# Norms, residuals and low parts of an fp32 encoder step on VectorE alone, with a norm's shift taken from its first tile and four gates moved into the projection

## The chip, the cores and the metric

The kernel runs on one core of a Trainium2 chip. Times are device microseconds of one launch on that core; the kernel before takes 1536.71 us (median of three runs, 1534.43 to 1537.71). Five engines matter: TensorE (PE, matmuls; PEld is its weight load), VectorE (DVE), ScalarE (ACT), GpSimd (POOL) and SyncE (SP, whose queue issues the loads and stores). They run side by side and wait for one another through semaphores; each takes its own instructions in the order in which the program has them.

## The reference

Two layers (DEPTH = 2) work on 320 tokens (64 of a running stream, 256 of a new one) of width 1024, all in fp32. Each layer is

```
x <- LN1(ALPHA*x + 0.5*FFN1(x))            FFN: silu(x @ w1a) * (x @ w1g) @ w2, hidden width 2816
z  = x @ w_in                              latent q, latent kv, rotary key, band q/k/v, gate_a, gate_b
A  = latent attention of z (8 heads), B = banded attention of z (8 heads)
mix = (sigmoid(gate_a)*(A @ w_proj_a) + sigmoid(gate_b)*(B @ w_proj_b)) @ w_out
x <- LN2(ALPHA*x + mix)
x <- LN3(ALPHA*x + 0.5*FFN2(x))
```

LN subtracts the mean over the 1024 features, divides by the root of the variance plus EPS, and applies a gain and a bias. The outputs are x and the new keys and values of both attentions.

## The kernel before, in words

Activations lie transposed: 1024 features are KD = 8 tiles of 128 partitions, the T = 320 tokens are columns. Every fp32 matmul of the weights is made of three products of a faster 32-bit type, fp32r: each operand is split into a high part (a rounded copy) and a low part (operand minus high part), and `mm3` (L126) adds hi x hi, hi x lo and lo x hi in PSUM.

Weights come as 383 chunks of 8 blocks (128x128 each), in the order in which the program asks for them (`WeightStream`, L49). SP loads a chunk of 512 KB into one of three staging buffers. `_split` (L71) makes the high part on ScalarE (L81) and the low part (L83), in pieces of 512 columns: every sixth low piece on GpSimd, the others on VectorE. There are four split buffers, and splits are asked for two chunks ahead. One chunk feeds 24 products.

A feed-forward stage (`ffn`, L255) makes 22 hidden tiles: two PSUM banks each, `evac` forms silu(a)*g, ScalarE its high part and GpSimd its low part (L276). Then `produce` (L290) makes the eight output tiles, which go straight into the norm.

`layer_norm` (L304) adds residual and product to eight tiles d. To keep the sum of squares accurate it first takes a shift c from all tiles: the mean over the features of the first NS = 4 tiles, through a matmul with a matrix of ones (pc, L369). After tile 4 (NB = 5) the shift is subtracted from the five tiles already there (L377); later tiles get it with their residual (L360). S collects the sum of the tiles (L347), Q the sum of squares (L353). GpSimd adds the halves of x (L315), scales them (L317) and does most of S and Q; VectorE the rest. For each finished tile `make_raw` (L323) forms high and low part of d times gain (L326, L327), because the next stage begins with the unnormalised tile: `group` opens six PSUM banks of the next stage, `step` adds one tile's products to all six, and the finished sums are corrected afterwards with mean and deviation (`finish`, L243). After the first `step` the sums of S and Q over partitions are two fp32 matmuls (pm, pq, L388 and L389); ScalarE and VectorE make the deviation (L398 to L405); GpSimd subtracts the mean from the eight tiles (L428), VectorE scales (L429), ScalarE writes the high part of the new x (L430) and VectorE the low part (L435, tile 7 on GpSimd). The last norm has no next stage; there the tiles go out to y (L407 to L421).

The mixer (`mixer`, L439; class `Mixer`, L469) has the banded attention first, then the latent one, head pair by head pair: `mla_scores` and `values` (L573). `M.run` (L115) gives the score and value products priority and keeps them in order among themselves. `gate` (L783) makes one tile of a gate: eight blocks of weights, 24 products, a tanh on ScalarE. `pb` (L885) multiplies gate b with a projected tile of the banded attention, whose outputs are the tiles ob. The outputs oa of the latent attention have the same tags (`o{n}{i}`, one buffer each, L840 and L906). `project` (L929) projects oa, multiplies with gate a, adds the gate b part and splits the sum; `w_out` and the norm follow. Tag K (keys, NK = 6 buffers) is shared by the banded keys, the latent keys, two pairs of gate a tiles (`gpair`, L788) and raw tiles of the norm.

PSUM has two tags, "mm" and "at", of four banks each. The order of instructions on every engine is not the order of the program: a planner (`schedule_with_timeline_sim`, L1050) runs the program on its own model of the engines' costs and gives each engine, at each time, the earliest instruction of the program that is ready in that model. Buffers are taken when their first writer is placed and are free when the last reader is done.

Of the kernel before, what the change touches and what calls it, by code (L numbers as in the profile page):

```python
# [14 lines left out]
P = 128  # L15
# [21 lines left out]
NK = 6  # L37
# [11 lines left out]
class WeightStream:  # L49


    def __init__(self, nc, dram, stage_pool, split_pool, ahead_dma, ahead_split):
        self.nc, self.dram = nc, dram
        self.sp, self.pp = stage_pool, split_pool
        self.ad, self.asp = ahead_dma, ahead_split
        self.order = []
        self.loaded = {}
        self.split = {}
        self.nl = self.ns = self.nlo = 0
# [11 lines left out]
    def _split(self):  # L71
# [6 lines left out]
        half = CH * P // (4 if c == 0 else 2)  # L78
        for a in range(0, n, half):
            b = min(n, a + half)  # L80
            self.nc.scalar.copy(hi[:, a:b], t[:, a:b])  # L81
            self.nlo += 1
            (self.nc.gpsimd if self.nlo % 6 == 0 else self.nc.vector).tensor_tensor(lo[:, a:b], t[:, a:b], hi.bitcast(F32)[:, a:b], ALU.subtract)  # L83
# [18 lines left out]
class Model:  # L102
# [152 lines left out]
    def ffn(self, l, f, pre):  # L255
# [3 lines left out]
        with tc.tile_pool(name="h", bufs=1, reuse_waits="tile") as hp, \  # L259
# [4 lines left out]
            def evac(p, pa, pg, raw):  # L264
# [11 lines left out]
                self.lo(hl[p], h, hh[p], eng=nc.gpsimd)  # L276
# [20 lines left out]
            tiles = [rp.tile([P, T], F32, name=f"d{m}") for m in range(KD + 3)]  # L297
# [4 lines left out]
            return self.layer_norm(l, which, tiles, raw, produce, 0.5, group)  # L302

    def layer_norm(self, l, which, tiles, raw, produce, ys, group):  # L304
# [4 lines left out]
        d, (c, S, Q) = tiles[:KD], tiles[KD:]  # L309
        NS, NB = 4, 5  # L310
        cg = l * NC_L + C_LN[which]
        cr = self.rr.tile([P, T], F32R, tag="cr", name="cr")

        def base(m):
            nc.gpsimd.tensor_tensor(d[m], self.xhi[m].bitcast(F32), self.xlo[m].bitcast(F32), ALU.add)  # L315
            if m < NB and ys != 1.0:
                nc.gpsimd.tensor_scalar(d[m], d[m], ALPHA, None, ALU.mult)  # L317
            if not last:
# [4 lines left out]
        def make_raw(m):  # L323
            if not last:
                g = self.cst[:, cg + 2 * m:cg + 2 * m + 1]
                nc.scalar.activation(raw[m][0][:, :T], d[m], AF.Copy, scale=g)  # L326
                nc.vector.scalar_tensor_tensor(raw[m][1][:, :T], d[m], g, raw[m][0].bitcast(F32)[:, :T], ALU.mult, ALU.subtract)  # L327

        def add(m, ps):
            if ys != 1.0:  # L330
                nc.vector.scalar_tensor_tensor(d[m], ps, ys, d[m], ALU.mult, ALU.add)
            elif m < NB:
                nc.vector.scalar_tensor_tensor(d[m], d[m], ALPHA, ps, ALU.mult, ALU.add)
            else:
                nc.vector.tensor_tensor(d[m], d[m], ps, ALU.add)  # L335

        def accumulate(m, ps):
            if m == KD - 1:
                if last:
                    nc.scalar.activation(sq, d[m], AF.Square)  # L340
                    return
                if ys != 1.0:
                    nc.vector.scalar_tensor_tensor(S, ps, ys, S, ALU.mult, ALU.add)
                else:
                    nc.vector.tensor_tensor(S, S, ps, ALU.add)
            elif m:
                nc.gpsimd.tensor_tensor(S, d[0] if m == 1 else S, d[m], ALU.add)  # L347
            if m == 0:
                nc.scalar.activation(Q, d[0], AF.Square)
            else:  # L350
                q = self.scratch("sq")
                nc.scalar.activation(q, d[m], AF.Square)
                (nc.gpsimd if m < NB else nc.vector).tensor_tensor(Q, Q, q, ALU.add)  # L353

        sq = self.scratch("sq") if last else None
        for m in range(KD):
            base(m)
        for m in range(KD):
            if m >= NB:
                nc.vector.scalar_tensor_tensor(d[m], d[m], ALPHA, c, ALU.mult, ALU.subtract)  # L360
                if m == KD - 1 and not last:
                    nc.gpsimd.tensor_tensor(S, S, d[m], ALU.add)
# [4 lines left out]
            if m == NB - 1:  # L367
                pc = self.psum("at", "pc")
                self.mm(pc[:, :T], self.ones if last else self.onesr, c if last else cr, True, True)  # L369
                nc.scalar.activation(c, pc[:, :T], AF.Copy, scale=float(KD) / NS)  # L370
            add(m, ps[:, :T])
            if m < NB:
                if 1 <= m < NS:
                    nc.gpsimd.tensor_tensor(cr if m == NS - 1 and not last else c, d[0] if m == 1 else c, d[m], ALU.add)
                if m == NB - 1:
                    for j in range(NB):
                        nc.vector.tensor_tensor(d[j], d[j], c, ALU.subtract)  # L377
                        accumulate(j, None)
                        make_raw(j)
            else:  # L380
                make_raw(m)
                accumulate(m, ps[:, :T])
        if not last:
# [4 lines left out]
        self.mm(pm[:, :T], self.ones, S, True, not last)  # L388
        self.mm(pq[:, :T], self.ones, Q, True, not last)  # L389
        if last:  # L390
            self.mm(pm[:, :T], self.ones, d[KD - 1], False, True)
# [7 lines left out]
        if last:  # L399
            nc.vector.scalar_tensor_tensor(v, pq[:, :T], EPS, msq, ALU.add, ALU.subtract)  # L400
        else:
            nc.vector.tensor_tensor(v, pq[:, :T], msq, ALU.subtract)
            nc.vector.tensor_scalar(v, v, 0.0, EPS, ALU.max, ALU.add)
        nc.scalar.activation(v, v, AF.Sqrt)
        nc.vector.reciprocal(v, v)  # L405
        if last:
            nc.scalar.copy(md, pm[:, :T])  # L407
            for m in (7, 2, 5, 6, 4, 0, 1, 3):
# [654 lines left out]
```

## Time and profile before

| | |
|---|---|
| median of three runs | 1536.71 us |
| profiled execution | 1536.8 us, of which the span is 1535.0 |
| TensorE busy | 1492.3 us (97%), 10207 products |
| VectorE busy | 900.1 us (59%) |
| ScalarE busy | 744.3 us (48%) |
| GpSimd busy | 564.5 us (37%) |
| DMA | 219.46 MB, 143 GB/s |

In the profile a line such as `L83 DVE TENSOR_TENSOR wlo<-wst,whi 128x512 ... x640 | 468.3, 762 | 444.1 <-ACT whi L81 439.4` names the line of the kernel, the engine, the operation, output and inputs by the program's names, their shapes and the number of such instructions; then the busy time in us and the mean of one in ns; then the engine's idle time just before them and what ended most of it. Many helpers record all their instructions under one line (all products are L109), so tiles tell them apart. In the mixer's norm the tiles d go by the name gt, because they take the buffers of gate b. Idle time of an engine that nobody waits for costs nothing.

### The profile page before, as it was taken

The numbers are of one execution on the slowest core, as the hardware profiler recorded it, in microseconds if no ns is written. First come the engines' busy times: TensorE is split into PE (matmuls) and PEld (weight loads), VectorE is DVE, ScalarE is ACT, GpSimd is POOL, SyncE is SP. The second block draws the span as 40 slices with busy tenths as digits, with TensorE's granted clock in tenths as the row PEclk, the third lists the DMA queues.
The fourth block names the chain that finished last, engine by engine and source line by source line (L and its number), as shares of the span: only waits on it lengthen the run. The fifth ranks groups of instructions, "written<-read, shape, count | busy, mean of one in ns | idle before, by whom it ended". The sixth has DMA issues, their size and how long they took to land. (4 is left out here: it accounts for less than half of the span.)

```text
span 1535.0 us, 26682 instructions
## 1 busy us (share of the span) xinstructions
PE 1492.3 (97%) x10207; PEld 1454.5 (95%) x10207; DVE 900.1 (59%) x1587; ACT 744.3 (48%) x1563; POOL 564.5 (37%) x602
## 2 busy tenths in 40 slices
PE   9999999999999899999999999999999998999996
PEld 9999999999898899999999999998998998999996
DVE  6333368675566994333884333786655579833345
ACT  5444345765453554443554443467645545544332
POOL 7322145332004683222483222452220156722234
PEclk9999999999999999999999999999999999999998
DMA  7545435844323435444434454458342333444441
GB/s 225 164 151 151 151 124 167 248 144 132 97 87 98 147 107 171 148 152 151 148 114 164 141 154 148 138 171 241 110 150 87 97 120 116 148 154 152 151 138 62
DMA packets 69921, 219.46 MB, mean 143 GB/s; under 512 B 8417, under 2 KB 17569, under 8 KB 69793
## 3 DMA queue, kind: packets, MB, share of 16 engines
q1 hardware_dynamic: 69792, 217.75, 45.6%
q8 instruction: 80, 1.31, 0.3%
q14 instruction: 49, 0.39, 0.1%
HBM read 211.74 MB, written 4.67 MB: 141 GB/s over the span
## 5 line engine op out<-in xcount | busy, mean ns | idle before, releaser
L83 DVE TENSOR_TENSOR wlo<-wst,whi 128x512 fp32r<-128x512 f32 (+1 forms) x640 | 468.3, 762 | 444.1 <-ACT whi L81 439.4
L81 ACT CAST whi<-wst 128x512 fp32r<-128x512 f32 (+1 forms) x768 | 437.0, 617 | 469.3 <-PE ps L109 189.1
L109 PE MATMUL ps<-xlo,whi 128*128 128x320 f32 x1760 | 547.5, 312 | 6.0 <-DVE xlo L435 6.0
L109 PE MATMUL ps<-xhi,whi 128*128 128x320 f32 x1760 | 548.0, 313 | 3.9 <-DVE fin L250 3.2
L109 PE MATMUL ps<-xhi,wlo 128*128 128x320 f32 x1760 | 545.6, 312 | 3.5 <-POOL wlo L83 3.2
L83 POOL TENSOR_TENSOR wlo<-wst,whi 128x512 fp32r<-128x512 f32 x128 | 176.1, 1376 | 466.3 <-ACT whi L81 428.8
L109 PEld LDWEIGHTS ps<-xlo,whi 128*128 128x128 f32 x1760 | 332.9, 189 | 7.2 <-DVE xlo L435 6.5
L109 PEld LDWEIGHTS ps<-xhi,whi 128*128 128x128 f32 x1760 | 332.9, 190 | 5.9 <-issue 4.1
L109 PEld LDWEIGHTS ps<-xhi,wlo 128*128 128x128 f32 x1760 | 332.3, 189 | 5.0 <-POOL wlo L83 3.4
L109 PE MATMUL ps<-hh,whi 128*128 128x320 f32 x704 | 217.8, 309 | 0.0
L109 PE MATMUL ps<-hh,wlo 128*128 128x320 f32 x704 | 217.6, 309 | 0.0
L109 PE MATMUL ps<-hl,whi 128*128 128x320 f32 x704 | 217.5, 309 | 0.0
L146 POOL TENSOR_TENSOR hl<-h,hh 128x320 fp32r<-128x320 f32 x88 | 86.1, 983 | 194.1 <-ACT hh L139 194.1
L109 PEld LDWEIGHTS ps<-hh,whi 128*128 128x128 f32 x704 | 132.1, 188 | 0.1
L109 PEld LDWEIGHTS ps<-hl,whi 128*128 128x128 f32 x704 | 132.1, 188 | 0.1
L109 PEld LDWEIGHTS ps<-hh,wlo 128*128 128x128 f32 x704 | 132.2, 188 | 0.0
L274 DVE TENSOR_TENSOR h<-silu,ps 128x320 f32<-128x320 f32 x79 | 38.3, 486 | 71.3 <-PE ps L109 67.4
L139 ACT CAST hh<-h 128x320 fp32r<-128x320 f32 x88 | 40.2, 457 | 54.3 <-DVE h L274 44.0
L109 PE MATMUL ps<-raw,whi 128*128 128x322 f32 x192 | 44.7, 319 | 1.2 <-DVE raw L327 1.2
L109 PE MATMUL ps<-rawl,whi 128*128 128x322 f32 x144 | 45.5, 316 | 0.0
L347 POOL TENSOR_TENSOR d<-d,d 128x320 f32<-128x320 f32 x24 | 27.0, 1125 | 50.0 <-DVE d L377 29.3
L109 PE MATMUL ps<-rawh,wlo 128*128 128x322 f32 x144 | 45.2, 314 | 0.0
(271 smaller groups left out, 2061.7 us busy)
## 6 DMA issues: line engine op xcount, KB each, us to landing
wst<-in_w_dram SPq DMA_DIRECT2D x382, 512.0 KB, 3.6
K<-in_ckT_dram SPq DMA_DIRECT2D x8, 256.0 KB, 5.2
vc<-in_cv_dram SPq DMA_DIRECT2D x8, 256.0 KB, 5.1
T<-in_E_dram SPq DMA_DIRECT2D x16, 128.0 KB, 4.5
xin<-in_x_dram SPq DMA_DIRECT2D x8, 160.0 KB, 6.1
out_kb_dram<-K SPq DMA_DIRECT2D x8, 160.0 KB, 4.0
out_vb_dram<-vt SPq DMA_DIRECT2D x8, 160.0 KB, 5.1
out_y_dram<-d SPq DMA_DIRECT2D x8, 160.0 KB, 1.8
```

Of the source, the lines that this page charges most:

```text
L81: self.nc.scalar.copy(hi[:, a:b], t[:, a:b])
L83: (self.nc.gpsimd if self.nlo % 6 == 0 else self.nc.vector).tensor_tensor(lo[:, a:b], t[:, a:b], hi.bitcast(F32)[:, a:b], ALU.subtract)
L109: return self.nc.tensor.matmul(out, lhsT, rhs, start=start, stop=stop)
L139: self.nc.scalar.copy(out, src)
L146: eng.tensor_tensor(out, src, hi.bitcast(F32), ALU.subtract)
L274: nc.vector.tensor_tensor(h, s, pg[:, :T], ALU.mult)
L347: nc.gpsimd.tensor_tensor(S, d[0] if m == 1 else S, d[m], ALU.add)
```

## The change

- `_split`: pieces are whole chunks of 1024 columns (but for the first two chunks), and all low parts are made on VectorE.
- `ffn`: the low part of the hidden tiles is made on VectorE.
- The residual (sum of the halves of x) is a step of its own, `residual`, into one wide tile d: on VectorE in the feed-forward stages, on GpSimd in the mixer, where it now stands in the middle of the attention and has a buffer of its own.
- `layer_norm`: everything is scaled by 1/ys (2 in the feed-forward stages, with EPS scaled by 4). The shift is taken from tile 0 alone, right after it: one ScalarE copy, one product with the ones, one ScalarE copy of the result. All other residuals get the shift at once, and each tile adds its product later. Sums S and Q are made on VectorE. After the sums VectorE subtracts the mean from PSUM; in the last norm GpSimd does it for tiles 4, 5 and 6. Every tile's end is done the same way.
- The mixer: pb for tiles 4 to 7 stands after the values of pair 2 (before: right after the first scores). Gates a 4 to 7 are made in `project`, between its tiles; their buffers are five of one tag, and tag K has five buffers (NK = 5).

```diff
-        half = CH * P // (4 if c == 0 else 2)
-        for a in range(0, n, half):
-            b = min(n, a + half)
+        piece = CH * P // (4 if c == 0 else 2 if c == 1 else 1)
+        for a in range(0, n, piece):
+            b = min(n, a + piece)
             self.nc.scalar.copy(hi[:, a:b], t[:, a:b])
-            self.nlo += 1
-            (self.nc.gpsimd if self.nlo % 6 == 0 else self.nc.vector).tensor_tensor(lo[:, a:b], ...)
+            self.nc.vector.tensor_tensor(lo[:, a:b], t[:, a:b], hi.bitcast(F32)[:, a:b], ALU.subtract)
...
-                self.lo(hl[p], h, hh[p], eng=nc.gpsimd)
+                self.lo(hl[p], h, hh[p])
...
+    def residual(self, d, eng):
+        for m in range(KD):
+            eng.tensor_tensor(d[:, m * T:m * T + T], self.xhi[m].bitcast(F32), self.xlo[m].bitcast(F32), ALU.add)
...
+        ps = produce(0)
+        nc.vector.scalar_tensor_tensor(d[0], d[0], scale, ps[:, :T], ALU.mult, ALU.add)
+        nc.scalar.copy(cr, d[0])
+        pc = self.psum("at", "pc")
+        self.mm(pc[:, :T], self.onesr, cr, True, True)
+        nc.scalar.activation(c, pc[:, :T], AF.Copy, scale=float(KD))
+        for m in range(1, KD):
+            nc.vector.scalar_tensor_tensor(d[m], d[m], scale, c, ALU.mult, ALU.subtract)
+        nc.vector.tensor_tensor(d[0], d[0], c, ALU.subtract)
+        finished(0)
+        for m in range(1, KD):
...
             ps = produce(m)
+            if m == KD - 1:
+                nc.vector.tensor_tensor(S, S, d[m], ALU.add)
+                nc.vector.tensor_tensor(S, S, ps[:, :T], ALU.add)
+            nc.vector.tensor_tensor(d[m], d[m], ps[:, :T], ALU.add)
+            if m < KD - 1:
+                nc.vector.tensor_tensor(S, d[0] if m == 1 else S, d[m], ALU.add)
+            finished(m)
...
+        for m in range(KD):
+            if last and m in (4, 5, 6):
+                nc.gpsimd.tensor_tensor(d[m], d[m], md, ALU.subtract)
+            else:
+                nc.vector.tensor_tensor(d[m], d[m], pm[:, :T], ALU.subtract)
+        for m in (0, 1, 2, 3, 7, 4, 5, 6) if last else range(KD):
+            g, b = gain[m]
+            nc.vector.scalar_tensor_tensor(d[m], d[m], g, v, ALU.mult, ALU.mult)
...
         mscores(0)
-        for m in range(8):
+        for m in range(4):
             pb(m)
...
         mvalues(2)
-        for m in range(3, 8):
-            ga[m] = self.gate(0, m)
+        self.d = self.tile([P, KD * T], F32, "d")
+        M.residual(self.d, nc.gpsimd)
+        for m in range(4, 8):
+            pb(m)
+        ga[3] = self.gate(0, 3)
         mvalues(3)
...
         for m in range(8):
+            later = {1: 4, 2: 5, 4: 6, 6: 7}.get(m)
+            if later:
+                self.ga[later] = self.gate(0, later)
             ps = self.proj("pa", m, self.oa)
```

`finished(m)` holds what `make_raw` and the squares did: ScalarE's high part and VectorE's low part of d times gain, ScalarE's square, and its sum into Q on VectorE.

More of the change, by code (lines that the diff above doesn't have):

```diff
@@ L295, in produce @@
                 return ps
-            tiles = [rp.tile([P, T], F32, name=f"d{m}") for m in range(KD + 3)]
+            d = rp.tile([P, KD * T], F32, name="d")
+            sums = [rp.tile([P, T], F32, name=n) for n in ("c", "S", "Q")]
+            self.residual(d, nc.vector)
             raw = group = None
@@ L349, in accumulate @@
                 nc.scalar.activation(Q, d[0], AF.Square)
-            else:
+            elif not (last and m == KD - 1):
                 q = self.scratch("sq")
                 nc.scalar.activation(q, d[m], AF.Square)
[L353 to L362, printed above, removed]
+                nc.vector.tensor_tensor(Q, Q, q, ALU.add)
@@ L366, in layer_norm @@
             ps = produce(m)
[L367 to L383, printed above, removed]
+            if m == KD - 1:
[5 more added lines that the diff above has]
+            finished(m)
+        sq = None
+        if last:
+            sq = self.scratch("sq")
+            nc.scalar.activation(sq, d[KD - 1], AF.Square)
+        else:
             grp, step = group()
@@ new lines, in layer_norm @@
+        if not last:
+            for k in range(1, KD):
+                step(k, raw[k], TR)
+        for m in range(KD):
+            if last and m in (4, 5, 6):
+                nc.gpsimd.tensor_tensor(d[m], d[m], md, ALU.subtract)
+            else:
+                nc.vector.tensor_tensor(d[m], d[m], pm[:, :T], ALU.subtract)
+        for m in (0, 1, 2, 3, 7, 4, 5, 6) if last else range(KD):
+            g, b = gain[m]
+            nc.vector.scalar_tensor_tensor(d[m], d[m], g, v, ALU.mult, ALU.mult)
+            if last:
+                nc.scalar.activation(d[m], d[m], AF.Identity, bias=b)
+                nc.sync.dma_start(out=self.a["y"][:, m, :], in_=d[m])
@@ L444, in mixer @@
             mix = u.project()
-            tiles = [u.tile([P, T], F32, f"gt1{m}") for m in range(KD)] + [u.tile([P, T], F32, f"gt0{m}") for m in range(3)]
+            sums = [u.tile([P, T], F32, f"gt1{m}") for m in range(3)]
             raw = [[u.tile([P, TR], F32R, f"o{n}{i}", 1, "raw") for n in "hl"] for i in range(NPAIR)]
@@ L464, in produce @@
                 return ps
-            return self.layer_norm(l, 2, tiles, raw, produce, 1.0, lambda: self.ffn_group(l, 2))
+            return self.layer_norm(l, 2, u.d, sums, raw, produce, 1.0, lambda: self.ffn_group(l, 2))
 class Mixer:
```

88 lines of the change are left out of this document (18 added, 70 removed).

## The prediction

> **What bounds the kernel now.** The first page says how far TensorE is from the span, and what VectorE and GpSimd carry.
>
> ```profile
> span 1535.0 us, 26682 instructions
> PE 1492.3 (97%) x10207; PEld 1454.5 (95%) x10207; DVE 900.1 (59%) x1587; ACT 744.3 (48%) x1563; POOL 564.5 (37%) x602
> ...
> L83 DVE TENSOR_TENSOR wlo<-wst,whi 128x512 fp32r<-128x512 f32 (+1 forms) x640 | 468.3, 762 | 444.1 <-ACT whi L81 439.4
> ...
> L83 POOL TENSOR_TENSOR wlo<-wst,whi 128x512 fp32r<-128x512 f32 x128 | 176.1, 1376 | 466.3 <-ACT whi L81 428.8
> ...
> L146 POOL TENSOR_TENSOR hl<-h,hh 128x320 fp32r<-128x320 f32 x88 | 86.1, 983 | 194.1 <-ACT hh L139 194.1
> ```
>
> TensorE works 97% of the span, so this change can only give back what TensorE loses: 1535.0 - 1492.3 = 42.7 us of idle time, and whatever it ran slowly. I therefore read the waits of TensorE next (columns: total us, times, longest).
>
> ```profile
> PE pm L109 <- DVE gt L345: 6.2, 2, 3.3
> PE ps L109 <- DVE xlo L435: 6.0, 2, 3.4
> PE ps L109 <- DVE fin L250: 3.2, 2, 1.7
> PE ps L109 <- POOL wlo L83: 3.2, 1, 3.2
> ...
> PE ps L109 <- DVE mxl L148: 1.8, 2, 1.5
> ...
> PE ps L109 <- DVE raw L327: 1.2, 2, 1.0
> ...
> PE ps L109 <- DVE wlo L83: 0.9, 1, 0.9
> ```
>
> Nearly all of it is lost to norm work: pm, xlo and raw (6.2 + 6.0 + 1.2 = 13.4 us) are the norm behind the mixer, once per layer; mxl and the one wlo on DVE (2.7 us) are the merged gates just before it; fin (3.2) is the start of the next stage. The view by windows shows the state around these gaps (columns: stretch, its length, busy us and instructions of PE, PEld, DVE, ACT, POOL, granted clock, DMA share, GB/s).
>
> ```profile
> 496.00:529.00 33.00, 27.93 (x186) 27.40 (x186) 32.09 (x42) 16.47 (x34) 21.22 (x18) 1.00 0.43 130
> 529.00:546.00 17.00, 13.64 (x87) 13.06 (x87) 15.28 (x21) 10.83 (x22) 9.46 (x9) 0.97 0.39 121
> 545.00:552.00 7.00, 5.72 (x21) 5.72 (x22) 7.00 (x17) 2.62 (x9) 5.03 (x6) 0.51 0.24 75
> 552.00:802.00 250.00, 250.00 (x1701) 249.68 (x1701) 141.74 (x220) 119.22 (x233) 112.25 (x118) 1.00 0.46 146
> 804.50:811.40 6.90, 5.71 (x21) 5.72 (x22) 2.23 (x3) 1.28 (x3) 6.90 (x9) 0.51 0.34 121
> 1289.00:1293.00 4.00, 4.00 (x17) 3.61 (x16) 2.04 (x5) 3.83 (x8) 1.77 (x2) 0.57 0.39 131
> 1306.00:1310.00 4.00, 3.88 (x16) 3.88 (x17) 4.00 (x10) 1.61 (x6) 3.61 (x3) 0.57 0.28 71
> ```
>
> Two readings. In the mixer norm of layer 0 (first two rows) VectorE is busy 32.09 of 33 us: here VectorE is the limit, though it is 59% busy on average. And four gaps were followed by a stretch at half the granted clock. At full clock a product costs 250/1701 = 0.147 us. The four stretches held 21, 21, 17 and 16 products in 5.72, 5.71, 4.00 and 3.88 us, that is 2.6 + 2.6 + 1.3 + 1.5 = 8.0 us lost (in the third, two fp32 products at 0.27 are allowed for).
>
> Why VectorE is late there: the same operation has very different prices (minimum/median/maximum in ns).
>
> ```profile
> L327 DVE SCALAR_TENSOR_TENSOR raw<-gt,cst,raw x16: 537/1159/1584, 515.2 to 1288.6; 128x320 fp32r<-128x320 f32 x16
> L377 DVE TENSOR_TENSOR gt<-gt,gt x10: 477/490/1172, 508.6 to 1269.9; 128x320 f32<-128x320 f32 x10
> L353 POOL TENSOR_TENSOR gt<-gt,sq x8: 1120/1129/1329, 511.7 to 1281.9; 128x320 f32<-128x320 f32 x8
> L353 DVE TENSOR_TENSOR gt<-gt,sq x6: 476/478/492, 527.4 to 1289.0; 128x320 f32<-128x320 f32 x6
> ```
>
> A two-input VectorE operation on SBUF takes 0.48 us when GpSimd is quiet and up to 1.58 us while GpSimd runs one; GpSimd itself needs 1.13. So work on GpSimd here is not free help, it slows VectorE. The chain of waits gives the undisturbed pace with consecutive operations overlapped (start, us, what):
>
> ```profile
> 1275.44 1.20 DVE wlo L83 x2
> ...
> 1287.65 0.41 DVE gt L345
> ```
>
> 0.60 us per 512 columns and 0.40 per 320, a slope of 0.2/192 = 1.04 ns a column, so a piece of 1024 takes about 0.60 + 0.53 = 1.13 us; two contended pieces, 2 x 0.76 = 1.52, bound it from above.
>
> **The change part by part.**
>
> *Low parts.* A chunk of weights feeds 24 products, 3.52 us. It costs VectorE 1.13 us instead of 5/6 x 2 x 0.76 = 1.27, and GpSimd nothing. The hl subtraction (88 times) goes from 0.98 on GpSimd to 0.40 on VectorE. In the feed-forward stages VectorE is busy 141.74 of 250 us, which covers both. The wait on GpSimd's wlo goes: -3.2 us (bounds -3.2 and 0, if VectorE were as late).
>
> *Mixer norm up to the sum.* New work of VectorE until S is complete: 1 + 7 residual steps, 1 shift of d0, 7 low parts, 6 squares, 6 adds, 8 sums = 36 operations x 0.40 = 14.4 us, and in the stretch of the first window row, 186 products or 27.3 us of TensorE, some 9 chunks x 1.13 = 10.2: 24.6 of 27.3 us. Before, GpSimd did 14 such steps there and slowed the rest. At 0.48 and 1.23 each (no overlap) it is 28.4, one us too late. So pm and raw, 6.2 + 1.2, shrink to between 0 and 2.2 over two layers. The new early matmul for the shift waits for one VectorE and one ScalarE step, about 1 us; the planner has the products of the next tile to run meanwhile, so nothing. Uncovered it is 1 us in each of six norms, 6 us.
>
> *Mixer norm after the sum.* GpSimd's eight subtractions stood in a row before the scaling (second row; the first, a group, is the reciprocal):
>
> ```profile
> L405 DVE RECIPROCAL rstd<-rstd 128x320 f32<-128x320 f32 x6 | 12.9, 2147 | 1.6 <-ACT rstd L404 1.6
> ...
> 533.05 7.96 POOL L428 TENSOR_TENSOR gt<-gt,md 128x320 f32<-128x320 f32 x8 [6.70 <-ACT md L423]
> ```
>
> Now VectorE does them from PSUM at 0.40 (3.2 us), partly while it waits for the square root. From pm, about 4.5 us to the reciprocal's end (it takes 2.15 us itself; two ScalarE and two VectorE steps of some 0.5 stand ahead of it), 3.2 of subtraction, 1.4 for the first tile, 5.9 for five chunks: the first xlo after 15 us, while TensorE has 126 products = 18.5 us. The 6.0 of xlo goes to 0 (bounds 0 and 2). The bank of pm stays taken until the eighth subtraction, some 8 us after pm; the next stage asks for it later than that, since it first runs the 18.5 us. I book -11.4 of 13.4 for raw, pm and xlo together.
>
> *Gates inside the projection.* Each tile there gave VectorE three steps:
>
> ```profile
> L148 DVE SCALAR_TENSOR_TENSOR mxl<-mx,mxh 128x320 fp32r<-128x320 f32 x16 | 11.9, 756 | 0.0
> L936 DVE TENSOR_TENSOR mx<-mx,gt 128x320 f32<-128x320 f32 x16 | 9.3, 591 | 0.0
> L935 DVE SCALAR_TENSOR_TENSOR mx<-gpair,ps 128x320 f32<-128x320 f32 x8 | 3.8, 474 | 0.0
> ```
>
> That is 1.82 us and half a chunk of wlo, against 12 products or 1.76 us of TensorE. Four gates of 3.52 us between them give it air: -2.7 for mxl and wlo (bounds -2.7 and 0). The gates' tanh and their weight chunks move with them; the number of chunks and loads is the same.
>
> *Next stage (fin).* VectorE gains some 2 us there against 3.2 us of added subtractions: -1.0 of 3.2 (bounds -3.2 and +1).
>
> *Attention.* This part can cost. TensorE is full here:
>
> ```profile
> 416.60:473.00 56.40, 56.40 (x454) 51.23 (x453) 31.39 (x95) 29.30 (x77) 5.27 (x11) 1.00 0.31 94
> ...
> 430.28 0.69 PE L109 MATMUL po<-pts,vc 128*64 128x64 f32 x16
> ...
> 435.68 0.81 PE L109 MATMUL sp<-K,Q 128*128 128x256 f32 x4
> ...
> 445.53 0.69 PE L109 MATMUL po<-pts,vc 128*64 128x64 f32 x16
> ```
>
> One head pair takes 445.53 - 430.28 = 15.2 us from values to values, a chain of softmax steps; independent products fill it. Before, seven gates stood there. After, four gates (14.1 us) leave for the projection and four pb tiles (48 products, 7.1 us) come in; two of the moved gates lie within the four split chunks and can be run ahead (7.1 us), which balances. Against it: ob and oa share buffers (tag o, one each), and pb 4 to 7 read ob after values 0 to 2 want to write oa. So ScalarE's and VectorE's reads of out wait for pb 7, and up to three of the four "at" banks stay taken. The second sp product (435.68) already came three us after the first. The larger pieces also block each softmax step a little longer. With NK at 5 the fourth band load follows scores 2 on SP's queue, weight loads behind it; 10 us of split weights cover that. I take 2.5 us of new gap per layer, +5.0 (bounds 0 and, in the rival below, far more). The eight residual steps on GpSimd find it idle: 5.27 of 56.40 us.
>
> *Last norm.* Its shift takes one fp32r product for two of 0.27, and pm has two fewer: -0.9. Behind it:
>
> ```profile
> 1522.24 5.45 POOL L412 TENSOR_TENSOR d<-d,md 128x320 f32<-128x320 f32 x6 [10.69 <-ACT md L407]
> 1522.34 0.87 DVE L410 TENSOR_TENSOR d<-d,pm 128x320 f32<-128x320 f32 x2
> ...
> 1525.32 5.33 DVE L419 SCALAR_TENSOR_TENSOR d<-d,cst,rstd 128x320 f32<-128x320 f32 x6
> ...
> 1529.82 1.74 POOL L417 TENSOR_SCALAR d<-d,cst 128x320 f32<-128x320 f32 x2
> 1530.20 1.03 ACT L420 ACTIVATE d<-d,cst 128x320 f32<-128x320 f32 x2 [0.51 <-DVE d L419]
> ```
>
> After the reciprocal (1525.3) VectorE has three subtractions left, 1.3 us, then eight tiles at ScalarE's pace of 0.52: 1525.3 + 1.3 + 0.5 + 4.2 = 1531.3, against 1531.56 now; the eight stores of y follow on SP's queue as before. Zero (bounds -1 and +1.5).
>
> *Clock.* If the gaps go, 8.0 us come back; I book -7.0. By these rows a gap of 2.6 us (xlo in layer 1) was followed by half clock and one of 2.9 (pm in layer 0) was not. The Trainium skill, "TensorE: Matmul & The Clock Gate", section "HAM oscillation — how this bites in real kernels", gives the rule that only gaps beyond about 3.4 us bring the half rate; by it small leftovers cost nothing and the full 8.0 would return, while by the 2.6 us row a leftover of that size could cost 1.5 more.
>
> **Sum.** -3.2 - 11.4 - 2.7 - 1.0 + 5.0 - 0.9 + 0 - 7.0 = -21.2. The profiled execution took 1536.8 (span plus 1.8), within 0.1 of the median 1536.71. 1536.8 - 21.2 = 1515.6, so 1516. Its own range is 1505 (every gap gone, all clock back, attention free: 3.2 + 13.4 + 2.7 + 3.2 + 8.0 + 0.9 = 31.4) to 1527 (half of the gain).
>
> **Rivals.**
>
> *VectorE stays the bound of the mixer norm.* It now does 39 steps where it did 28. If the pace is 0.55 and not 0.40, it is late as before and pm and xlo keep their 12.2 us and 3 of the clock's: -21.2 + 11.4 + 3 = -6.8, 1530. For it: 32.09 of 33 us busy. Against: L353 on DVE at 478 with GpSimd quiet.
>
> *Attention runs dry (slower).* One mechanism: values 0 to 2 hold their banks until pb 7, so the scores and values of the last two pairs run one after the other with nothing beside them. The same stretch for the tile ps alone:
>
> ```profile
> 416.60:473.00 56.40, 43.11 (x270) 39.08 (x269) 5.43 (x11) 8.97 (x24) 1.00 0.31 94
> ```
>
> 270 products of fill, 39.7 us at 0.147; the other 16.7 belong to three scores and four values, some 5 us a pair. Uncovered, a pair costs 15.2 - 5 = 10 us. Two pairs in two layers are 40, four long gaps some 10 of clock: 1515.6 - 5 + 50 = 1561. It decides above (21.2 + 5)/2 = 13 us per layer; around that the time is unchanged. For it: one buffer per o tile, four banks, a 15 us chain. Against: pb 4 to 7 need nothing from oa, so a planner that takes what is ready runs them early, and 0 us were idle here before.
>
> *The gaps only move.* The gates and residuals end the mixer later or the new shift is not covered (6 us), fin grows by 1 in both layers, and the clock stays at its 8: about 1536.
>
> **How the numbers follow.** Forecast 0.54, VectorE bound 0.14, better than 1505 0.03, gaps only move 0.09, attention dry 0.20, of which 0.02 ends near no change. A measurement here tells 0.2% (3 us) from nothing. Faster 0.71, same 0.11, slower 0.18. The range 1503 to 1546 leaves out most of the dry case, 0.13, and 0.02 below.
>
> **What would show it.** No PE wait on wlo of POOL, pm, mxl and xlo under 1 us; 640 wlo pieces become some 390 of about 1.2 us; L327's median falls from 1159 to near 540; no half-clock stretch in the norms. I am wrong if the window of the last head pairs shows PE idle for more than 5 us a layer, or if VectorE is still 97% busy before pm.

## The result, and the profile after

The kernel after takes 1524.98 us (median of four runs, 1522.48 to 1527.07), the kernel before on the same chip 1536.3 us. The ratio is 0.9926, with a 95% interval from 0.9907 to 0.9946: faster, by 11.3 us where 20.7 were forecast. The profiled execution took 1524.2 us, of which the span is 1522.4.

The first page of the kernel after:

```profile
span 1522.4 us, 25515 instructions
PE 1488.9 (98%) x10204; PEld 1453.5 (95%) x10204; DVE 932.7 (61%) x1571; ACT 713.4 (47%) x1190; POOL 105.6 (7%) x194
```

GpSimd went from 564.5 us to 105.6, and VectorE, which took that work, rose only from 900.1 to 932.7. TensorE's idle time fell from 42.7 us to 1522.4 - 1488.9 = 33.5. The waits of TensorE in the kernel after (total us, times, longest):

```profile
PE ps L108 <- DVE xlo L405: 6.7, 6, 3.1
PE ps L108 <- DVE fin L249: 5.8, 3, 2.8
PE ps L108 <- ACT xhi L404: 5.5, 2, 3.8
PE po L108 <- ACT pt L562: 2.2, 2, 1.1
```

Gone are the waits for pm, raw, mxl and both kinds of wlo. But 18.0 us now stand in three rows for one thing, the normalised tiles of a norm and the group that follows it: xlo was 6.0, fin was 3.2, and xhi is new. By place, the mixer norms have 6.9 us of them in layer 0 and 4.5 in layer 1. The other 3.4 and 3.3 us stand behind the first feed-forward norm of each layer, where the kernel before waited 1.7 and 1.6 us, for fin alone. The stretches behind these waits, by windows (columns as in the prediction's window table):

```profile
265.30:272.20 6.90, 5.22 (x18) 4.85 (x19) 6.90 (x14) 2.74 (x7) 5.12 (x5) 0.51 0.90 278
541.80:548.70 6.90, 4.29 (x16) 4.29 (x17) 6.90 (x16) 4.19 (x8) 0.00 (x0) 0.51 0.00 1
1023.00:1026.60 3.60, 3.60 (x17) 3.60 (x16) 3.60 (x9) 2.00 (x4) 2.53 (x6) 0.53 0.06 16
1292.70:1299.70 7.00, 5.20 (x19) 4.94 (x20) 7.00 (x17) 2.40 (x8) 0.00 (x0) 0.51 0.24 76
```

Four stretches at half clock again: 18, 16, 17 and 19 products in 5.22, 4.29, 3.60 and 5.20 us cost 2.6 + 1.9 + 1.1 + 2.4 = 8.0 us over 0.147 a product, which is what the four of before cost. Two of them lie at new places: 265 and 1023 us are the ends of the first feed-forward norm of each layer, where the kernel before had none. (One more such stretch, in the last norm, stands in both kernels.)

To see where the time went I compare the two traces by TensorE's products, which are the same but for three in the last norm: the time between the start of the n-th and of the m-th product. (Worked out from the start times in the traces; a few products change places at the cuts, worth some 0.3 us.)

| products | what lies there | before | after | difference |
|---|---|---|---|---|
| 0 to 300 | first tiles | 47.5 | 46.3 | -1.3 |
| 300 to 1500 | feed-forward, layer 0 | 176.0 | 176.0 | 0 |
| 1500 to 1860 | first norm, into the mixer | 55.3 | 59.8 | +4.5 |
| 1860 to 3300 | attention | 201.0 | 199.4 | -1.6 |
| 3300 to 3900 | projection and mixer norm | 102.5 | 98.0 | -4.4 |
| 3900 to 6600 | two feed-forward stages, the norm between | 402.7 | 396.7 | -6.0 |
| 6600 to 6960 | first norm of layer 1 | 55.4 | 59.7 | +4.3 |
| 6960 to 9300 | mixer and its norm, layer 1 | 346.1 | 339.6 | -6.6 |
| 9300 to the end | last stage, last norm | 147.6 | 146.0 | -1.6 |

The sum is -12.6, as the spans say. The change gained 21.4 us at six places and lost 8.8 us at two, the edges behind the first feed-forward norms. There the prediction had booked a small gain, its term for fin.

### The profile page after: what moved, and what is told of

Same layout as the page of the kernel before. It is cut to its first block, busy times and chain, and to the rows that moved or that the text cites. A ratio compares the mean times of both kernels' runs of the same rounds, so it can differ in the third digit from the quotient of the medians.

```text
span 1522.4 us, 25515 instructions
## 1 busy us (share of the span) xinstructions
PE 1488.9 (98%) x10204; PEld 1453.5 (95%) x10204; DVE 932.7 (61%) x1571; ACT 713.4 (47%) x1190; POOL 105.6 (7%) x194
## 4 chain that ended last, share of the span: by engine, by line
PE 95%; DVE 3%; ACT 1%; issue 0%; DMA 0%; ACTq 0%; DVEq 0%
PE ps L108 89%; PE sp L108 1%; PE po L108 1%; PE ss L108 1%; DVE d L399 1%; DVE wlo L82 1%; DVE xlo L405 1%; PE st L549 0%; DVE rstd L387 0%; ACT d L401 0%; DVE d L396 0%; DMA wst<-in_w_dram 0%; PE pt L556 0%; PE st L552 0%; PE pt L555 0%
## 5 line engine op out<-in xcount | busy, mean ns | idle before, releaser
L82 DVE TENSOR_TENSOR wlo<-wst,whi 128x1024 fp32r<-128x1024 f32 (+1 forms) x387 | 471.7, 1220 | 384.6 <-ACT whi L81 382.9
L81 ACT CAST whi<-wst 128x1024 fp32r<-128x1024 f32 (+1 forms) x387 | 402.4, 1041 | 495.4 <-PE ps L108 233.6
L145 DVE TENSOR_TENSOR hl<-h,hh 128x320 fp32r<-128x320 f32 x88 | 42.5, 488 | 17.5 <-ACT hh L138 17.4
L272 ACT ACTIVATE silu<-ps 128x320 f32<-128x320 f32 x79 | 33.9, 433 | 25.7 <-PE ps L108 25.7
L108 PE MATMUL ps<-rawh,whi 128*128 128x322 f32 x144 | 45.4, 315 | 0.0
```

Of the source, the lines that this page charges most:

```text
L82: self.nc.vector.tensor_tensor(lo[:, a:b], t[:, a:b], hi.bitcast(F32)[:, a:b], ALU.subtract)
L108: return self.nc.tensor.matmul(out, lhsT, rhs, start=start, stop=stop)
L145: eng.tensor_tensor(out, src, hi.bitcast(F32), ALU.subtract)
L272: nc.scalar.activation(s, pa[:, :T], AF.Silu)
```

## The experiments

Ratios are to the kernel before on the same chip; the run of the kernel after gives 0.9926 [0.9907, 0.9946]. Times of the same batch can be compared directly, times of different batches by their ratios.

### Low parts alone

The kernel before with all low parts on VectorE, first in pieces of 512 columns:

```diff
-            (self.nc.gpsimd if self.nlo % 6 == 0 else self.nc.vector).tensor_tensor(lo[:, a:b], ...)
+            self.nc.vector.tensor_tensor(lo[:, a:b], ...)
...
-                self.lo(hl[p], h, hh[p], eng=nc.gpsimd)
+                self.lo(hl[p], h, hh[p])
```

> The kernel before with one part of the change alone: all low parts (of weights and of hidden tiles) on VectorE, pieces still 512 columns. Theory A (GpSimd's weight pieces cost time only where TensorE waited for one): the 3.2 us wait on GpSimd's piece and the 2.6 us of half clock behind it go, the mixer norm keeps its waits on pm, xlo and raw of about 13 us, 1529 to 1532 us. Rival B (the low parts are the whole gain of the change, since VectorE is slowed by GpSimd everywhere): 1525 us, and pm's wait falls under 2 us.

Measured: 1525.31 us, ratio 0.9948 [0.9933, 0.9963]: between the theories. The wait on GpSimd's piece is gone, and pm's fell to 1.8 us, as B asks; but 5.9 us for xlo and 3.4 for raw stay, as A says. Then the same in pieces of 1024:

```diff
-        half = CH * P // (4 if c == 0 else 2)
+        half = CH * P // (4 if c == 0 else 2 if c == 1 else 1)
```

> The kernel before with nothing but the low parts changed: all on VectorE, and in pieces of 1024 columns as in the kernel after (the run with pieces of 512 took 1525.31 us, ratio 0.9948). Theory A, the size of the pieces is a part of the gain: one whole piece costs VectorE 1.22 us and two half ones 1.46 us, so that a chain of six chunks behind a norm's sum is 1.5 us shorter; over six norms up to 8 us with the half-clock stretches that this shortens: 1519 to 1523. Theory B, the size is worth nothing, since a whole piece comes later by as much as it is cheaper: 1524 to 1526.

Measured: 1525.33 us, ratio 0.9933 [0.9909, 0.9956]: theory B. The intervals overlap, so the size of the pieces is worth nothing that can be told. Products 3900 to 6600 take 396.7 us in both, 6.0 less than before: the wait on GpSimd's low part at 802 us is gone, with its half-clock stretch. But what matters most in the run with 1024 is the edge that the kernel after had made worse. Products 1500 to 1860 take 54.3 us there and 59.8 in the kernel after, with VectorE's low parts of the weights the same. So the loss at that edge comes from the norms or the mixer, not from the low parts.

### Norms alone

The kernel after with the low parts of the kernel before: the diff above, the other way round. (So it holds the moves in the mixer as well as the new norms.)

> The kernel after with the low parts as before (pieces of 512, every sixth on GpSimd, low halves of the hidden activations on GpSimd). Theory A, the two halves of the change add up: the low parts alone took 8.4 us of the 11.3 us off, so norms, gates and attention are worth 2.9 us: 1532 to 1534. Theory B, the norms alone carry the removal of the waits for raw parts and mean (13.4 us in the kernel before) and the low parts' gain overlaps with it: 1525 to 1529. Theory C, the norms on VectorE lengthen its queue while GpSimd's low parts still slow it down: 1537 or more.

Measured: 1519.26 us, ratio 0.9893 [0.9869, 0.9918]: faster than any of the three theories said. The gains of the two halves, 0.7% and 1.1%, do not add up to 0.7%; they overlap, and joining them seems to have cost something (the intervals of this run and of the kernel after still overlap a little; a later pair of runs shows it again). The overlap is easy to see: products 3900 to 6600 take 396.7 us here too, although GpSimd still makes every sixth half piece of wlo. At 802 us in the kernel before, that piece (one half piece, 1.34 us) stood in GpSimd's queue behind scaling steps of the norm and the low part of a hidden tile:

```profile
800.92 1.47 POOL L317 TENSOR_SCALAR d<-d 128x320 f32<-128x320 f32 x1
802.35 0.18 POOL L321 CAST rawl<-cstl 128x2 fp32r<-128x2 f32 x1
802.49 0.86 POOL L146 TENSOR_TENSOR hl<-h,hh 128x320 fp32r<-128x320 f32 x1
803.32 1.01 POOL L317 TENSOR_SCALAR d<-d 128x320 f32<-128x320 f32 x1
804.29 1.34 POOL L83 TENSOR_TENSOR wlo<-wst,whi 128x512 fp32r<-128x512 f32 x1
```

Take the norm's work off GpSimd or take the low part off it: either one removes that wait, and only once. The edges of the first norms are slow here as well (60.5 and 58.1 us).

### Attention: the held banks, and the gates

The prediction had booked 5 us for banks that values 0 to 2 hold until the last pb. Put back, all eight pb stand right after the first scores:

```diff
-        for m in range(4):
+        for m in range(8):
             pb(m)
...
-        for m in range(4, 8):
-            pb(m)
```

> The changed kernel with pb of tiles 4 to 7 back right behind tiles 0 to 3, so that ob is read before the first values write oa. Theory A (the banks held for 21 us cost nothing, because the chain of the head pairs sets the pace): same within 3 us of the changed kernel's 1525. Rival B (holding the banks lengthens the chain by some us per layer, which later gates hide only partly): 2 to 5 us faster, 1520 to 1523.

Measured: 1525.39 us, ratio 0.9945 [0.993, 0.9959]. No gain, theory A; a new wait of 0.5 us per layer for the casts of oh. And the gates 3 to 7 put back ahead of the last values:

```diff
-        ga[3] = self.gate(0, 3)
+        for m in range(3, 8):
+            ga[m] = self.gate(0, m)
...
-            later = {1: 4, 2: 5, 4: 6, 6: 7}.get(m)
-            if later:
-                self.ga[later] = self.gate(0, later)
```

> The changed kernel with gates 3 to 7 made ahead of the last values again and none inside the projection (eight gate buffers). Theory A (the gates give VectorE air in the projection): the waits on mxl and wlo come back, 2 to 4 us per two layers, and VectorE enters the norm later, so pm, xhi and xlo wait longer: 1528 to 1533 us. Rival B (with GpSimd quiet the projection's VectorE steps fit without the gates): 1524 to 1526 us, no wait on mxl over 0.5 us.

Measured: 1525.98 us, ratio 0.9948 [0.9931, 0.9965]: theory B. The waits that came back in the projection are 0.4 us (wlo) and 0.3 (whi). Both ratios lie 0.2% (3 us) above that of the kernel after, with intervals that overlap it, so neither move is worth anything that these runs can tell from nothing. TensorE has no idle time in the last head pairs of layer 0, with the banks held (the kernel after, below) or not (58.00 of 58.00 us busy in the run with pb back):

```profile
410.00:468.00 58.00, 58.00 (x465) 52.66 (x464) 34.91 (x93) 26.93 (x66) 0.92 (x6) 1.00 0.29 86
```

### The subtractions of the mean

After the mean's product VectorE did eight subtractions (3.27 us) ahead of the variance, in the mixer norm of layer 0 although the sum of squares was there. Three runs tried them: on GpSimd as before, behind the reciprocal, and left out.

```diff
-            if last and m in (4, 5, 6):
+            if not last or m in (4, 5, 6):
                 nc.gpsimd.tensor_tensor(d[m], d[m], md, ALU.subtract)
```

> The changed kernel with one part undone: after the sums GpSimd subtracts the mean from the eight tiles again (from the SBUF copy md), VectorE does the rest. Theory A (the eight subtractions on VectorE, 3.3 us ahead of the variance, are what makes xhi, xlo and fin late): the waits on xhi, xlo and fin, 18.0 us together, fall by 6 us or more, 1517 to 1520 us. Rival B (VectorE was late before the sum already, and GpSimd's subtraction slows its scaling): waits as now or longer, 1525 to 1530 us.

Measured: 1522.66 us, ratio 0.9926 [0.9908, 0.9944], the same as the kernel after, and between the theories. The waits: fin 8.4, xlo 6.5, xhi 2.5, together 17.4 us where 18.0 were.

```diff
-        nc.vector.reciprocal(v, v)
+        rec = nc.vector.reciprocal(v, v)
...
-                nc.vector.tensor_tensor(d[m], d[m], pm[:, :T], ALU.subtract)
+                ins = nc.vector.tensor_tensor(d[m], d[m], pm[:, :T], ALU.subtract)
+                if not last:
+                    self.order(ins, rec)
```

> The kernel after with the eight subtractions of the mean (3.3 us of VectorE) ordered behind the reciprocal in the five norms that are not the last. Theory A, they delay the variance and so the first normalised tile: the waits for xhi, xlo and fin fall from 18 us to 8 to 12, and with them some of the four half-clock stretches: 1514 to 1520. Theory B, in four of the five norms VectorE would only wait for the sum of squares in that time, and what comes after the reciprocal grows by as much: waits of 16 us or more, 1523 to 1528.

Measured: 1530.78 us, ratio 0.9974 [0.9961, 0.9986]: slower than the kernel after by some 0.5%, beyond what theory B said; the waits for xlo, fin, xhi and u are 20.9 us. The timeline of VectorE in the first norm of this run:

```profile
245.86 0.49 DVE L384 TENSOR_TENSOR rstd<-pq,msq 128x320 f32<-128x320 f32 x1 [1.32 <-PE pq L108]
...
249.10 2.15 DVE L387 RECIPROCAL rstd<-rstd 128x320 f32<-128x320 f32 x1
251.17 3.21 DVE L396 TENSOR_TENSOR d<-d,pm 128x320 f32<-128x320 f32 x8
```

VectorE now idles 1.32 us for the sum of squares, the reciprocal ends at 251.25 (251.68 in the kernel after), and the subtractions come on top. The planner's order, subtractions first, was the better one: they fill a wait.

```diff
-            else:
+            elif last:
                 nc.vector.tensor_tensor(d[m], d[m], pm[:, :T], ALU.subtract)
```

> The kernel after with the eight subtractions of the mean left out in the five norms that are not the last (the normalised tiles are then not centred; this only takes 3.3 us of VectorE's work out of each). Theory A, VectorE's backlog between the mean and the normalised tiles sets the waits: each norm's chain is 3.3 us shorter, waits of 18 us fall to 3 to 6 us, and the half-clock stretches (8 us) with them: 1502 to 1510. Theory B, the subtractions fill time in which VectorE waits for the sum of squares: waits stay over 13 us, 1520 to 1525.

Measured: 1519.10 us, ratio 0.9892 [0.9862, 0.9921], so leaving out 16 us of VectorE's work bought some 5 us, with intervals that overlap; waits of 8.4 us for fin, 4.4 for xlo and 1.6 for xhi remain. Theory B by the waits, a little below its range by the time. The subtractions are not the main thing that makes the norms end late.

### The residual steps on GpSimd

What is different at the edge of the first norm shows on two engines side by side. GpSimd in the kernel after (start, us, what), then VectorE at the same time:

```profile
258.20 7.20 POOL L307 TENSOR_TENSOR d<-xhi,xlo 128x320 f32<-128x320 f32 x6 [18.46 <-DVE xlo L405]
265.83 2.98 POOL L307 TENSOR_TENSOR d<-xhi,xlo 128x320 f32<-128x320 f32 x2 [0.43 <-DVE u L246]
```

```profile
256.37 1.22 DVE L82 TENSOR_TENSOR wlo<-wst,whi 128x1024 fp32r<-128x1024 f32 x1
257.51 5.36 DVE L405 SCALAR_TENSOR_TENSOR xlo<-d,cst,xhi 128x320 fp32r<-128x320 f32 x6
262.79 0.15 DVE L246 TENSOR_SCALAR u<-ps 128x1 f32<-128x1 f32 x1
262.86 1.82 DVE L82 TENSOR_TENSOR wlo<-wst,whi 128x1024 fp32r<-128x1024 f32 x1
```

The program has the mixer's residual steps in the middle of its attention. Their inputs are xhi and xlo and their buffer is now their own, so the planner starts them on an idle GpSimd as soon as the first xlo is written, 235 us before anyone needs them (their first reader, L341, runs at 493.77 us), and beside the very instructions that TensorE waits for. Each xlo then takes 0.89 us (5.36 over six). The test leaves every operation as it is and only orders these steps behind a GpSimd step of the attention:

```diff
-        nc.gpsimd.tensor_tensor(out, r, t, ALU.add)
+        self.roped = nc.gpsimd.tensor_tensor(out, r, t, ALU.add)
...
-        M.residual(self.d, nc.gpsimd)
+        M.residual(self.d, nc.gpsimd, self.roped)
```

(`residual` then orders each of its steps behind that instruction.)

> The kernel after with the mixer's eight residual steps on GpSimd ordered behind the last GpSimd step of the rotation (that one ended at 364 us in layer 0). In the kernel after they started at 258 us, as soon as the first low part xlo was there, and while they ran six xlo took 0.89 us each on VectorE. In the run with the old norms and the low parts on VectorE, GpSimd was idle there, an xlo took 0.61 us and the stall behind was 0.7 us, where it is 2.2 + 1.2 us now. Theory A, these steps slow the low parts at the end of the first feed-forward norm of each layer: the mean of xlo falls from 708 ns to 550 to 620 ns, the wait for xlo at 263 us and at 1015 us goes, each of the two edges gets 3 to 4 us shorter: 1516 to 1519. Theory B, VectorE's own added work (residual, sums, subtraction) sets this edge: 1523 to 1526.

Measured: 1514.50 us, ratio 0.9888 [0.9871, 0.9906]. Theory A, and 1.5 us more than it asked. GpSimd and VectorE in this run:

```profile
359.07 8.71 POOL L307 TENSOR_TENSOR d<-xhi,xlo 128x320 f32<-128x320 f32 x8
```

```profile
257.27 2.87 DVE L407 SCALAR_TENSOR_TENSOR xlo<-d,cst,xhi 128x320 fp32r<-128x320 f32 x6
260.05 0.16 DVE L246 TENSOR_SCALAR u<-ps 128x1 f32<-128x1 f32 x1
260.12 1.22 DVE L82 TENSOR_TENSOR wlo<-wst,whi 128x1024 fp32r<-128x1024 f32 x1
```

Six xlo in 2.87 us instead of 5.36, a chunk of wlo in 1.22 instead of 1.82. Products 1500 to 1860 take 54.8 us (59.8), products 6600 to 6960 54.1 (59.7): both edges are better than those of the kernel before, and the half-clock stretches at 265 and 1023 us are gone. The Trainium skill, "SBUF — State Buffer", section "SBUF: two separate sides", says that a GpSimd operation that reads SBUF and a VectorE operation with two SBUF inputs lock each other out for a whole instruction; the xlo at nearly twice its time agrees with it in kind.

The same on the kernel with the norms alone:

> The same late residual steps on the kernel with the new norms and the old low parts (1519.26 us). Theory A: its edges behind the first feed-forward norms had cost 134.9 and 93.7 us for 900 and 600 products, 4.5 us each over the run with the old norms; 3 to 4.5 us of each go: 1510 to 1514. Theory B: 1518 to 1521.

Measured in the same batch: 1510.36 us, ratio 0.9852 [0.9834, 0.9869]. Theory A again. That it is 4.1 us below the other one says that the low parts on VectorE, worth 0.7% with the old norms, cost about 0.3% with the new ones. Where: products 3300 to 3900, projection and mixer norm, take 96.1 us here and 98.4 there. TensorE also takes the mean's product of that norm earlier here, after 72 of its 144 raw products and not after 88.

### The shift and the mean in TensorE's order

What is left are the mixer norms. VectorE in the kernel after, layer 0: ahead of the shift, and from the end of the sum to the first xlo.

```profile
493.77 0.49 DVE L341 SCALAR_TENSOR_TENSOR d<-d,ps 128x320 f32<-128x320 f32 x1
498.50 0.89 DVE L347 SCALAR_TENSOR_TENSOR d<-d,gt 128x320 f32<-128x320 f32 x2 [4.24 <-ACT gt L345]
...
523.10 0.49 DVE L357 TENSOR_TENSOR gt<-gt,ps 128x320 f32<-128x320 f32 x1
...
528.88 3.27 DVE L396 TENSOR_TENSOR d<-d,pm 128x320 f32<-128x320 f32 x8
532.07 0.48 DVE L384 TENSOR_TENSOR rstd<-pq,msq 128x320 f32<-128x320 f32 x1
532.47 1.22 DVE L82 TENSOR_TENSOR wlo<-wst,whi 128x1024 fp32r<-128x1024 f32 x1
...
535.03 2.14 DVE L387 RECIPROCAL rstd<-rstd 128x320 f32<-128x320 f32 x1
...
539.31 3.78 DVE L399 SCALAR_TENSOR_TENSOR d<-d,cst,rstd 128x320 f32<-128x320 f32 x8
...
543.81 0.55 DVE L405 SCALAR_TENSOR_TENSOR xlo<-d,cst,xhi 128x320 fp32r<-128x320 f32 x1
```

And TensorE's two products:

```profile
497.69 0.31 PE L108 MATMUL pc<-cr,onesr 128*128 128x320 f32 x1
...
527.15 0.70 PE L108 MATMUL pm<-gt,ones 128*128 128x320 f32 x2
```

VectorE has d0 at 494.26, and then nothing to do for 4.24 us, in the stage in which it is the limit: the shift's operand, a ScalarE copy, is there at 494.75, and its product comes 2.9 us later, behind 20 others. S is complete at 523.59, but TensorE takes the mean's product at 527.15, after 88 of the 144 raw products. Only 56 are left (8.2 us), and the first xlo comes 16.7 us later. The last two runs move these two products forward in TensorE's order. First, on the kernel with late residual steps:

```diff
+        self.shift = self.mm(pc[:, :T], self.onesr, cr, True, True)
...
+                    self.behind = self.shift if m == 2 and k >= 2 else None
                     self.mm3(ps[:, :T], w, mix[k], k == 0, k == KD - 1)
...
+        mean = self.mm(pm[:, :T], self.ones, S, True, True)
...
             for k in range(1, KD):
+                self.behind = mean if k >= 4 else None
                 step(k, raw[k], TR)
```

(`mm` orders a product behind `self.behind`, where that is set.)

> The kernel after with the late residual steps, and in the mixer's norm TensorE's shift product ordered ahead of the third tile's products from its third block on (it came after 27 products, 2.9 us later than its operand), and the mean's product ahead of the raw products from the fifth tile on (it came after 88, 3.6 us after S was complete). Theory A, what ends these norms late is where these two products stand in TensorE's order: VectorE's 4.24 us of idling ahead of the shift falls to 1.5, the mean comes 2 to 5 us earlier, and the waits behind the mixer's norm (6.9 and 4.5 us) fall by 2 to 4 us each, with some of the half-clock stretches: 4 to 9 us below the run with the late residual steps alone. Theory B, TensorE only waits at these two products instead: within 1.5 us of that run.

Measured: 1511.86 us, ratio 0.9865 [0.985, 0.9881], 2.6 us below the run with late residual steps: between the theories. The shift did not move at all, since the planner put products of other tiles ahead of it, and VectorE still idles 4.24 us; the mean came after 72 raw products. So this run tested only the mean, and only in layer 0: there the waits behind the mixer norm fell from 6.3 us to 4.2, while in layer 1, where the mean hardly moved (from 73 to 72), they stayed at 4.5. The last run takes the norms alone with late residual steps. It orders the second and third tile from the fourth block on, and all later tiles, behind the shift, and puts the mean earlier:

```diff
-                    self.behind = self.shift if m == 2 and k >= 2 else None
+                    self.behind = self.shift if m > 2 or k >= 3 else None
...
-                self.behind = mean if k >= 4 else None
+                self.behind = mean if k >= 3 else None
```

> The kernel with the new norms, the old low parts and the late residual steps (1510.36 us), and in the mixer's norm now all products of the later tiles from the third block on ordered behind the shift's product (before this only the third tile's were, and the shift kept its place, 2.9 us behind its operand), and the raw products from the fourth tile on behind the mean's product, which then comes after 31 raw products instead of 72 in layer 0 and after 24 instead of 63 in layer 1. Theory A, the places of these two products in TensorE's order set how late the mixer's norm ends: VectorE's idle 4.24 us ahead of the shift falls below 2.5, and the waits behind the norm (3.6 and 2.8 us) shrink more than the waits at the two products grow: 1504 to 1508. Theory B, TensorE waits for S at the mean's product about as long as it waited behind the norm: 1509 to 1512. Theory C, it waits longer, at both: over 1512.

Measured: 1501.49 us (five runs, 1501.3 to 1501.87), ratio 0.9792 [0.9778, 0.9806]: theory A, and better than its range. The waits of TensorE in the run that it builds on, the norms alone with late residual steps:

```profile
PE ps L109 <- DVE fin L250: 4.5, 3, 3.0
PE ps L109 <- DVE xlo L408: 3.5, 2, 2.8
```

And in this one:

```profile
PE pc L111 <- ACT cr L350: 2.5, 2, 1.5
PE po L111 <- ACT pt L574: 2.2, 2, 1.1
PE ps L111 <- DVE fin L255: 1.5, 2, 0.8
```

VectorE ahead of the shift, and the mean's product:

```profile
488.77 0.48 DVE L349 SCALAR_TENSOR_TENSOR d<-d,ps 128x320 f32<-128x320 f32 x1
490.72 2.91 DVE L355 SCALAR_TENSOR_TENSOR d<-d,gt 128x320 f32<-128x320 f32 x7 [1.47 <-ACT gt L353]
```

```profile
515.75 0.70 PE L111 MATMUL pm<-gt,ones 128*128 128x320 f32 x2
```

TensorE now waits for the shift, 1.06 us in layer 0 and 1.48 in layer 1, and that is a good trade: VectorE's idle time falls from 4.24 to 1.47, 113 raw products stand behind the mean in layer 0 instead of 72 (56 in the kernel after), the waits for xhi, xlo and fin behind both mixer norms are gone, and so is every half-clock stretch between the start and the last norm. Products 3300 to 3900 take 90.1 us instead of 96.1, 6960 to 9300 334.0 instead of 338.4. This is the fastest version, by 2.1% of the kernel before. It moves both products at once, so what each of them is worth in it was not told apart. What the late residual steps and the new order give with all low parts on VectorE was not tried.

## Why the prediction was right, and where it was not

The direction and the range held; of the 21.2 us of the sum, 12.6 came. That the range held says little, since 1503 to 1546 takes in no change at all. Nearly the whole miss lies in one term: at the edges of the first norms -1.0 was booked and +8.8 came. The rest comes to -21.4 where -20.2 were booked, in part by luck: attention's +5.0 did not come, and the mixers fell 5.9 short of the rest.

*Low parts, -3.2.* Right: the wait is gone, 640 pieces on VectorE and 128 on GpSimd became 387 of 1220 ns, and a chunk's step from one start to the next is 1.14 us (256.37 to 257.51) where 1.13 was taken. The stretch 3900 to 6600 gave 6.0, which is 3.2 and the 2.6 of clock behind it. The norms alone give the same 6.0, so the change paid for this one twice. With the norms of before, the low parts alone gave more than that, 8 to 10 us by the ratios, since the waits for pm, mxl and fin shrank with them. The first tiles gave 1.3 that were not in the sum.

*Mixer norm up to the sum.* The waits for pm and raw went, as booked, and the low part of raw fell from a median of 1159 ns to the 540 that was named:

```profile
L332 DVE SCALAR_TENSOR_TENSOR raw<-d,cst,raw x16: 545/547/553, 505.6 to 1276.3; 128x320 fp32r<-128x320 f32 x16
```

But VectorE took 29.8 us from d0's step to S (493.77 to 523.59) where 24.6 were worked out, and the step that failed is "the planner has the products of the next tile to run meanwhile, so nothing". For TensorE it was nothing. VectorE, the limit of this stage, stood still for those 4.24 us, and no term of the sum had that.

*Mixer norm after the sum, the 6.0 of xlo to 0.* Wrong. The chain from pm to the first xlo was 16.7 us where 15 were worked out. The cover failed: "TensorE has 126 products = 18.5 us" took the mean's place from the program, behind 18 raw products. The planner puts it by its own reckoning of when S will be ready, and it came after 88. The trace of the kernel before could have told: there the mean of the mixer norms comes after 63 and 62 raw products. So the wait for pm turned into waits for xhi, xlo and fin: 3.8 + 3.1 us in layer 0, 1.7 + 2.8 in layer 1, 11.4 us for the 13.4 of before. The run that moved the mean alone took 2.1 us off these waits in layer 0, and the last run, which restores the cover (and moves the shift too), has none of them left.

*Gates, -2.7.* The waits for mxl and wlo went. But putting the gates back returns only 0.7 us of waits. The gates took little of it: in the run with the low parts alone, where they stand as before, mxl is down from 1.8 us to 0.2 and wlo from 0.9 to 0.6.

*Next stage, fin -1.0.* Wrong in sign. The 3.2 us of before are the edges of the first norms; there the kernel after waits 6.7 us, 3.0 for fin and the rest for xlo at 263 and 1015 us, and the edges got 8.8 us longer over two layers with the half clock. (The other 2.8 of fin's 5.8 us are those of the mixer norm above.) The step that failed is "The eight residual steps on GpSimd find it idle". GpSimd was idle; but they ran where VectorE was needed, not where the program has them. The prediction had quoted the price of just that (up to 1.58 us for an operation of 0.48), and did not ask when the moved steps would start.

*Attention, +5.0.* Did not come: the stretch got 1.6 us shorter, and putting the pb back changed nothing. What was argued against the rival, that the planner runs what is ready, speaks against this smaller term as well. This miss hid others: for both mixers with their norms and clock the sum has +5.0 - 11.4 - 2.7 - 4.4 = -13.5 (4.4 is the clock's 7.0 without the 2.6 behind the wait at 802), and they gave -12.6. Without the attention term the forecast there would have been 5.9 too good.

*Last norm and tail, -0.9 and 0.* -1.6 together, within the bounds.

*Clock, -7.0.* On balance nothing came back: 2.6 us did behind the wait at 802 us and 1.1 behind the mixer norms, and the new edges took 3.7. The two edges and the two mixer norms are four places with waits, and four stretches. The rule that the prediction cites from the Trainium skill ("TensorE: Matmul & The Clock Gate", section "HAM oscillation — how this bites in real kernels"), that only gaps beyond about 3.4 us bring the half rate, did not hold here. At 1015 to 1021 us there are four gaps of 0.37 and one of 1.8, and half clock follows at 1023.

(Half of the sum's gain is 1526, not the 1527 of its range; nothing hangs on it.) Of the signs that the prediction named, two failed: a wait for xlo of 3.1 us where none over 1 was to be, and half clock in the norms. Of the rivals, "The gaps only move" was right in kind for the mixer norms (11.4 of 13.4 us) and the clock (8.0 of 8.0). "VectorE stays the bound of the mixer norm" was half right: it was late (busy 26.31 of 28.70 us from the shift to the mean), but by its place in the order and not by its pace.

```profile
498.50:527.20 28.70, 28.70 (x197) 28.70 (x196) 26.31 (x47) 18.05 (x28) 0.00 (x0) 1.00 0.49 152
```

## What to carry to other kernels

A step that is moved to an idle engine starts when its inputs and its buffer are ready, not where the program has it: ask what runs beside it then, and order it behind something if that is on the path. Where a planner fills the queues, the cover of a chain is what stands behind its start in the built order, so look up the place of the product that starts it; a wait of 1 us on the busiest engine can be cheaper than 4 us of idling on the one that sets the stage. And two remedies for one wait pay once.

## What was not expected of the hardware

- The same eight GpSimd steps take 8.71 us at 359 us, with three VectorE steps beside them, and 7.20 + 2.98 = 10.2 us beside VectorE's xlo, and VectorE pays more than GpSimd: 2.5 us on six xlo (2.87 to 5.36) and 0.6 on a piece of wlo.
- Half clock came behind gaps of at most 1.8 us (layer 1, at 1015 us), and not behind a single gap of 1.06 or 1.48 us (the last run). The stretches between the start and the last norm are 3.41 us long, or two or three times that (10.2 with the late residual steps), and they start whole multiples of 3.41 us apart: in the kernel after at 265.37, 541.85, 1023.12 and 1292.78 us. In the 3.41 us just ahead of these four, TensorE was idle for 1.7, 2.6, 1.8 and 2.8 us. So what counts seems to be the idle part of one such step and not the length of a gap. That fits the two rows that the prediction could not join: in the kernel before, the gap of 2.9 us lies across two steps, with 1.7 and 1.3 us in each, and the gap of 2.6 us in one. The traces give no sharp limit; in the kernel after, a step with 1.7 us idle (at 535 us) was not followed by half clock.
